# An encoder layer on one core: where the first maxima of the attention are taken, how the Fourier branch's second half is run, and which engine does the last norm

## The chip, the core and the metric

The kernel runs on one core of a Trainium2 chip. Five engines work from their own queues and meet through semaphores: TensorE (PE) multiplies matrices, VectorE (DVE) and ScalarE (ACT) do elementwise work and reductions, GpSimd (POOL) elementwise work on SBUF, and SyncE (SP) issues most DMAs. The metric is the device time of one execution in microseconds (us); less is better.

## What is computed

Two sequences of 2048 tokens ("prompt" and "sample"), 1024 wide, go through one layer with shared weights:

```python
u = _rmsnorm(h, g_norm)
z = u @ w_in                       # q | k | v | attention gate | Fourier input | Fourier gate
q = _apply_axial_rope(_rmsnorm(q, g_q), cos, sin)
k = _apply_axial_rope(_rmsnorm(k, g_k), cos, sin)
a = _blocked_gqa(q, k, v) * jax.nn.silu(ga)        # 8 q heads, 2 kv heads of 64
fo = _fourier_branch(f, w_fmix) * jax.nn.silu(gf)  # real part of a 2-D DFT, then a map per group
h = h + jnp.concatenate([a, fo], axis=-1) @ w_out
gate = jax.nn.sigmoid(_rmsnorm(h, g_ple) @ w_ple_gate)
h = h + (p @ w_ple) * gate
y = _rmsnorm(h, g_final)
```

## The kernel before

Products that need the accuracy are done as three matmuls of 16-bit halves (`mm`, L428); the attention's product with v and the DFT are done in 32 bits.

**Projections** (`project`, to about 847 us). The tokens of both sequences come in 16 chunks of 256, the prompt's eight first. `iteration(i)` issues for several chunks at once: loads and norm of a later chunk, q, k and v of this one, rotations of earlier ones, and `sweep_part`, which takes the Fourier and gate products of a chunk piece by piece (some 66 pieces). After each fifth piece it takes one step of a background generator `bg` (weights of the later stages). `bank()` hands out PSUM banks, five from the pool `psX` and three from `psF`. Orders are written out by hand: what is issued first on an engine runs first there. In this stage `self.dq` is None, so work given to `defer` is issued at once. In iteration 13 (`n - 3`), `early()` closes a pool and starts the attention generator, which loads k and v of the prompt's first kv head and the q of two units (L1076 to L1090).

**Attention** (`attention`). A unit is 128 queries of one kv head with its four q heads: 64 units, 8 steps each. Step `g` begins with `flush`, which issues what was deferred; then come the scores of step `j` of unit `u` (six matmuls on PE, L1104, two exponentials on ACT, L1107, a running sum of 128x1024 on POOL, L1112); one maximum of a unit 13 steps ahead (`maxima`: a pair of matmuls into `ps_m`, which has one buffer, L1127, and a reduction on DVE, L1131); and on each fourth step the product with v (L1162). `negate` and `max_rows` turn the eight maxima of a unit into a row (L1148) that is subtracted by the first score matmul. Because of the 13 steps (`AHEAD`), the loop starts at `g = -13`, and in the first 13 steps there is nothing but maxima.

**Fill.** `interleave` runs attention, and after each of its steps takes pieces of a second generator, `fill`, as far as a budget goes: 755 us in all, spread over the steps, with at most 5 us saved up. A piece that yields None ends the turn. The fill is the second half of the Fourier branch (`fourier2`, eight tiles for a sequence), then the output part (`outp`, 32 tiles of 128 tokens). In a tile of `fourier2`, g (g_in), gate (gf_in) and constants are loaded two tiles ahead; PE transforms over positions (L1025) and over channels (`mix`, L983), ACT copies, DVE adds and subtracts (L993), POOL multiplies by the gate (L995), and `fin`, deferred by two steps, takes the largest value on DVE (`fmax`, L999) and stores the result (`fod`, L941). `fmax` of a sequence sets a scale (`mix_max`) that the output part needs. The tiles g_in, gf_in and fo share 14 buffers. `fourier2` was called once for each sequence; each call begins with loads and three empty steps and ends when its deferred work is out (`after(self.tick, 1)`). `hook` loads one piece of the output weights twice a tile.

In `outp`, tile t is multiplied by w_out (`out1`), normed (`norm`: 16 small operations on POOL, L1363 to L1366), transposed (`out2`, which needs the norm), multiplied by the gate's weights (`out3`) and, two tiles later, scaled and stored (`out4`, L1373 on DVE and L1375 as a DMA issued by POOL). `out4` was handed to the slow queue at the seventh piece of `out3`, `out2` right after it. A tile may be prepared only when both kv heads' units of its tokens are done (`ready`).

**End.** After the last attention step the rest of the fill runs alone, `self.dq` is None again, and work is issued at once.

`defer(fn)` runs `fn` at the next flush; nested once more, it runs two flushes later. `after(ticket, more)` yields None until that flush and `more` others are over.

Of the kernel before, what the change touches and what calls it, by code (L numbers as in the profile page):

```python
# [19 lines left out]
DM = 1024  # L20
# [119 lines left out]
class Build:  # L140
    def __init__(self, ctx, tc, a, y):
# [9 lines left out]
        self.slow, self.passed, self.step = [], set(), 0  # L151
        self.nw2k = 10
# [388 lines left out]
    def project(self, P, PU, W, early, wkv, wq, wga, bg, mid):  # L541
# [216 lines left out]
        def iteration(i):  # L758
# [41 lines left out]
            if i == n + 3:  # L800
                self.drain(bg)
                for f in stores_next:
# [131 lines left out]
    def fourier2(self, s, pool, hook=lambda: None):  # L934
# [5 lines left out]
        def tiles(dma, t, y, dram, sb, load):  # L940
# [9 lines left out]
        def load_c(t):  # L950
            C[t] = pool.tile([128, 2, 128], F32, name="c2", bufs=FP + 1)
            nc.sync.dma_start(C[t][:].rearrange("p g c -> p (g c)"), self.a["c_dft2"][t])

        def load_g(t, g):
            G[t, g] = w2k("g_in")
            r = 16 * t + 8 * g
            nc.sync.dma_start(G[t, g][:], self.gd[s][r:r + 8].rearrange("r t d -> (r t) d"))
# [5 lines left out]
        def loads(t):  # L963

            if t < 8:
                todo.extend([lambda: load_c(t), lambda: load_g(t, 0), lambda: load_g(t, 1)])
            if 0 <= t - 1 < 8:
# [7 lines left out]
        def mix(t, fT, fx):  # L975
# [21 lines left out]
            def fin():  # L997
                for y in range(2):
                    nc.vector.tensor_reduce(out=self.fmax[s][:, 2 * t + y:2 * t + y + 1], in_=fo[y][:], op=ALU.max,  # L999
# [4 lines left out]
            self.tick = self.defer(lambda: self.defer(fin))  # L1004
# [12 lines left out]
        for t in range(8):  # L1017
# [17 lines left out]
            if t == 0:  # L1035
# [10 lines left out]
        yield from self.after(self.tick, 1)  # L1046
# [15 lines left out]
    def attention(self, kvp):  # L1062
# [9 lines left out]
        def load_kv(s, kv, pool):  # L1072
            for b in range(2):
                k = pool.tile([128, 4, 3, 128], F16, name="k", bufs=2)
# [3 lines left out]
            for b in range(2):  # L1078
                v = pool.tile([128, 8, 64], F32, name="v", bufs=2)
# [40 lines left out]
        def maxima(u, k):  # L1120
# [3 lines left out]
            ps = self.psM.tile([128, 1024], F32, name="ps_m")  # L1124
            for c in range(2):
                sl = slice(64 * c, 64 * c + 64)
                nc.tensor.matmul(ps[:, c * 512:(c + 1) * 512], Q[u][0][sl, h, :], kt[s, kv, half][sl, :, 0, :],  # L1127
                                 start=True, stop=True)
            if k == 0:
                MX[u] = st.tile([128, 4, 2], F32, name="a_mx", bufs=2)  # L1130
            nc.vector.reduce_max(MX[u][:, h, half:half + 1], ps[:], axis=AX.X)  # L1131
# [4 lines left out]
            nc.vector.tensor_reduce(out=m[:], in_=mx[:], op=ALU.max, axis=AX.X)  # L1136
# [7 lines left out]
        def max_rows(u):  # L1144
# [4 lines left out]
            MR[u] = mr = pool.tile([128, 4, 128], F16, name="mr", bufs=1)  # L1149
# [58 lines left out]
        load_kv(0, 0, kvp)  # L1208
        for u in range(2):
            load_q(u)  # L1210
        pool = yield 0.0
        nms = [pool.tile([128, 128], F32, name=f"nm{i}", bufs=1) for i in range(2)]
        for x in nms:
            nc.gpsimd.memset(x[:], 0.0)
        ones = pool.tile([128, 64], F32, name="ones", bufs=1)
        nc.gpsimd.memset(ones[:], 1.0)
        kone = pool.tile([128, 128], F16, name="kone", bufs=1)
        nc.gpsimd.memset(kone[:], K_ONE)
        own = pool.tile([128, 4], F32, name="own", bufs=1)
        nc.gpsimd.tensor_tensor(out=own[:], in0=self.ident[:, 0:4], in1=self.ident[:, 64:68], op=ALU.add)  # L1220
        load_kv(0, 1, pool)
        fresh = {last[0, kv]: (kv, p) for kv, p in enumerate((kvp, pool))}
        for g in range(-AHEAD, 8 * n + 7):
# [5 lines left out]
            if j == 4 and u - 1 in fresh:  # L1229
                load_kv(1, *fresh[u - 1])  # L1230
            if 0 <= u < n:
                scores(u, j)
            v, k = divmod(g + AHEAD, 8)
            if v < n:
                maxima(v, k)
            if k == 1 and 0 <= v - 1 < n:
                negate(v - 1)
# [450 lines left out]
```

## Time and profile before

| what | us |
|---|---|
| median of 3 runs | 2833.74 (2832.60 to 2834.88) |
| the profiled execution | 2832.63 |
| its span, first to last instruction | 2830.9 |
| mean granted TensorE clock | 0.982 of full speed |

The span is cut into stretches by what runs: projections to 847.2 us, the 13 lead steps to 898.0, attention with the Fourier fill to about 1045, attention with the output fill to 2748, the end of the fill to 2814.7, and 16.2 us after the last matmul. A row of a table by stretches gives for each engine the time it was busy and in brackets the number of its instructions. In an order of time, the bracket behind an instruction is the idle time of its engine just before it and what ended it. A wait is shown as "engine, what waited, <- what it waited for: us in total, times, longest".

### The profile page before, as it was taken

The numbers are of one execution on the slowest core, as the hardware profiler recorded it, in microseconds if no ns is written. First come the engines' busy times: TensorE is split into PE (matmuls) and PEld (weight loads), VectorE is DVE, ScalarE is ACT, GpSimd is POOL, SyncE is SP. The second block draws the span as 40 slices with busy tenths as digits, with TensorE's granted clock in tenths as the row PEclk, the third lists the DMA queues.
The fourth block names the chain that finished last, engine by engine and source line by source line (L and its number), as shares of the span: only waits on it lengthen the run. The fifth ranks groups of instructions, "written<-read, shape, count | busy, mean of one in ns | idle before, by whom it ended". The sixth has DMA issues, their size and how long they took to land.

```text
span 2830.9 us, 40445 instructions
## 1 busy us (share of the span) xinstructions
PE 2692.4 (95%) x15332; PEld 1190.8 (42%) x15332; DVE 1687.5 (60%) x2397; ACT 1211.3 (43%) x2047; POOL 1648.4 (58%) x1462
## 2 busy tenths in 40 slices
PE   5699999999996998999999999999999999999997
PEld 2356565655555443333333333333333333333333
DVE  7555566563445565666666666666666666666632
ACT  4333343332222454554444455444444444444441
POOL 0122333242342787777776778777776777777663
PEclk9899999999997999999999999999999999999999
DMA  7376777773439542112221223322222222222222
GB/s 217 97 207 176 198 214 182 181 182 88 130 85 327 166 129 68 51 53 73 65 59 41 66 55 83 97 60 51 75 56 65 58 70 73 53 73 70 58 58 80
DMA packets 418532, 296.43 MB, mean 105 GB/s; under 512 B 259456, under 2 KB 360128, under 8 KB 418336
## 3 DMA queue, kind: packets, MB, share of 16 engines
q1 hardware_dynamic: 405280, 251.55, 33.7%
q0 software_dynamic: 13056, 42.29, 4.2%
q8 instruction: 120, 1.97, 0.3%
q14 instruction: 76, 0.62, 0.1%
HBM read 149.56 MB, written 86.51 MB: 83 GB/s over the span
## 4 chain that ended last, share of the span: by engine, by line
PE 83%; DVE 5%; DMA 3%; issue 3%; ACT 2%; POOL 2%; SPq 1%; POOLq 0%; ACTq 0%; DVEq 0%
PE ps_f L428 34%; PE ps_o L1162 15%; PE ps_x L428 14%; PE ps_s L1104 13%; PE ps_m L1127 4%; PE ps_f L1196 1%; ACT p L1107 1%; PE ps_f L1148 1%; PE ps_f L1025 1%; POOL acc L1112 1%; PE ps_f L983 1%; PE ps_x L884 1%; DVE a_mx L1131 1%; DVE w_mx L299 0%; DVE mh L1314 0%
## 5 line engine op out<-in xcount | busy, mean ns | idle before, releaser
L1112 POOL TENSOR_TENSOR acc<-acc,p 128x1024 f32<-128x1024 f32 x384 | 913.7, 2379 | 225.9 <-ACT p L1107 171.2
L1131 DVE TENSOR_REDUCE a_mx<-ps_m 128x1 f32<-128x1024 f32 x512 | 626.0, 1223 | 593.2 <-PE ps_m L1127 592.4
L1107 ACT ACTIVATE p<-ps_s,s_scale 128x512 f32<-128x512 f32 x1024 | 647.5, 683 | 754.8 <-PE ps_s L1104 735.1
L1162 PE MATMUL ps_o<-p,v 128*64 128x512 f32 x2048 | 466.3, 597 | 0.0
L428 PEld LDWEIGHTS <-uc 128*128 128x128 f16 x3072 | 302.7, 99 | 338.1 <-DMA uc<-hl 37.8
L1104 PE MATMUL ps_s<-q,k 64*128 64x512 f16 x3072 | 432.1, 381 | 11.3 <-ACT p L1107 10.9
L428 PE MATMUL ps_f<-w_pg,hT 128*128 128x512 f16 x1464 | 350.5, 380 | 2.3 <-DMA hT<-h_hl 2.2
L1104 PEld LDWEIGHTS <-k 64*128 64x128 f16 x3072 | 118.6, 94 | 317.3 <-issue 246.7
L1162 PEld LDWEIGHTS ps_o<-p,v 128*64 128x64 f32 x2048 | 141.8, 137 | 257.8 <-issue 248.8
L1110 POOL TENSOR_TENSOR acc<-p,p 128x1024 f32<-128x1024 f32 x64 | 150.4, 2350 | 153.7 <-ACT p L1107 153.4
L428 PEld LDWEIGHTS <-hT 128*128 128x128 f16 x1536 | 138.5, 98 | 205.6 <-issue 60.8
L1127 PE MATMUL ps_m<-k,q 64*128 64x512 f16 x1024 | 200.7, 380 | 24.3 <-DVE a_mx L1131 23.8
L428 PE MATMUL ps_f<-w_wo,mh 128*128 128x512 f16 x744 | 181.6, 382 | 5.0 <-DVE mh L1314 5.0
L428 PE MATMUL ps_f<-w_wo,mT 128*128 128x512 f16 x744 | 180.1, 380 | 1.5 <-DMA mT<-mh 1.5
L428 PEld LDWEIGHTS <-w_ga 128*128 128x128 f16 x1536 | 149.9, 98 | 38.0 <-ACT w_ga L321 9.0
L901 POOL DMA_DIRECT2D gfd<-gt x32 | 19.4, 606 | 222.6 <-DVE gt L929 217.9
L1178 ACT ACTIVATE tb<-ps_o,a_scale 64x256 f32<-64x256 f32 x128 | 60.0, 469 | 169.2 <-PE ps_o L1162 168.4
L1198 DVE RECIPROCAL ps_f<-ps_f 128x256 f32<-128x256 f32 x64 | 112.4, 1756 | 12.3 <-PE ps_f L1196 12.3
L919 POOL DMA_DIRECT2D agd<-gat x64 | 35.2, 550 | 137.8 <-DVE gat L929 133.3
L428 PEld LDWEIGHTS <-mh 128*128 128x128 f16 x768 | 68.4, 98 | 111.3 <-issue 37.1
L428 PEld LDWEIGHTS <-mT 128*128 128x128 f16 x768 | 70.6, 98 | 100.1 <-issue 22.5
L428 PE MATMUL ps_x<-uc,w_ga 128*128 128x256 f16 x1008 | 112.7, 273 | 0.0
(273 smaller groups left out, 3337.2 us busy)
## 6 DMA issues: line engine op xcount, KB each, us to landing
q<-qTd SPq DMA_DIRECT2D x256, 64.0 KB, 2.2
ag<-agd SPq DMA_DIRECT2D x64, 256.0 KB, 3.2
out<-h POOLq DMA_DIRECT2D x32, 512.0 KB, 3.2
x<-in_x_prompt SPq DMA_DIRECT2D x16, 512.0 KB, 4.6
w_st<-in_w_out SPq DMA_DIRECT2D x32, 256.0 KB, 3.8
gfd<-gt POOLq DMA_DIRECT2D x32, 256.0 KB, 3.0
gd<-ge POOLq DMA_DIRECT2D x32, 256.0 KB, 3.8
agd<-gat POOLq DMA_DIRECT2D x64, 128.0 KB, 2.6
```

Of the source, the lines that this page charges most:

```text
L428: self.nc.tensor.matmul(ps, lhs(ia, k), rhs(ib, k), start=(i == 0), stop=(i == 3 * ks - 1))
L884: nc.tensor.matmul(pf[:], self.dft1[:] if t % 8 else self.dft1x[:, t // 8], F.pop(tt)[:], start=True, stop=True)
L919: nc.gpsimd.dma_start(self.agd[s][1, r * 128:(r + 1) * 128, c * n:(c + 1) * n], gt[:, :n])
L1104: nc.tensor.matmul(S[u][e][:], w[sl], q[sl].rearrange("p h q -> p (h q)"), start=j == i == 0, stop=i + 1 == len(todo), skip_group_check=True)
L1107: nc.scalar.activation(p[:, e, :], S[u][e][:], AF.Exp, scale=self.sc["s_scale"][:])
L1110: nc.gpsimd.tensor_tensor(out=ACC[u][:], in0=P[u, 0][:], in1=p[:], op=ALU.add)
L1112: nc.gpsimd.tensor_tensor(out=ACC[u][:], in0=ACC[u][:], in1=p[:], op=ALU.add)
L1127: nc.tensor.matmul(ps[:, c * 512:(c + 1) * 512], Q[u][0][sl, h, :], kt[s, kv, half][sl, :, 0, :], start=True, stop=True)
L1131: nc.vector.reduce_max(MX[u][:, h, half:half + 1], ps[:], axis=AX.X)
L1162: nc.tensor.matmul(o[64 * e:64 * e + 64, :], vt[s, kv, c // 8][:, c % 8, :], p[:, e, :], start=(j == 0), stop=(j == 7))
L1178: nc.scalar.activation(tb[64 * e:64 * e + 64], ov[64 - 64 * e:128 - 64 * e, e], AF.Copy, scale=self.sc["a_scale"][64 - 64 * e:128 - 64 * e ...
L1198: nc.vector.reciprocal(r, ps[:, 0:256])
```

## The change

- The 13 leading maxima are a generator `leads`, kept as `self.ahead`. `sweep_part` takes one step of it at every piece whose count leaves 2 when divided by 5; what is left is taken in iteration `n + 3`. A first maximum uses two banks of `psX` instead of `ps_m`, and two reductions of 512 instead of one of 1024; between its matmuls and its reductions the generator yields. The attention loop starts at `g = 0`.
- For that, k and v of both kv heads, the units' rows and small constants lie in the pool opened by `early()`, and k and v of the second head are loaded there in iteration 13.
- `fourier2` runs 16 tiles, eight of each sequence, in one call; at tile 10, when the first sequence's last `fin` is over, it yields "half", and `fill` makes the output generator. `fin` is deferred by four steps instead of two. `hook` loads one piece of the weights a tile instead of two.
- In `outp`, while attention runs, `out4` and `out2` of a tile wait until more than three flushes have passed since its `norm`.
- When attention is over, `norm` runs on DVE; the last tile is scaled in two halves, each stored by a DMA that SP issues.
- The number of steps for which the budget is spread is 13 less.

```diff
@@ sweep_part, in project
                         if len(done) % NBF == 0:
                             next(bg, None)
+                        if len(done) % NBF == 2:
+                            next(self.ahead, None)
@@ fourier2
-            self.tick = self.defer(lambda: self.defer(fin))
+            self.tick = self.defer(lambda: self.defer(lambda: self.defer(lambda: self.defer(fin))))
...
-        for t in range(8):
+        for t in range(16):
+            if t == 10:
+                yield from self.after(half, 3)
+                yield "half"
...
-            if t == 0:
+            if t % 8 == 0:
+                if t:
+                    half = self.tick
...
-        yield from self.after(self.tick, 1)
+        yield from self.after(self.tick, 3)
@@ attention
-        def maxima(u, k):
+        def maxima(u, k, first=False):
...
-            ps = self.psM.tile([128, 1024], F32, name="ps_m")
+            if first:
+                ps = [self.psX.tile([128, 512], F32, name="ps_x")[:] for _ in range(2)]
+            else:
+                pm = self.psM.tile([128, 1024], F32, name="ps_m")
+                ps = [pm[:, c * 512:(c + 1) * 512] for c in range(2)]
...
-            nc.vector.reduce_max(MX[u][:, h, half:half + 1], ps[:], axis=AX.X)
+            if first:
+                yield
+            for c, x in enumerate(ps if first else [pm[:]]):
+                nc.vector.reduce_max(MX[u][:, h, half, c:c + 1], x, axis=AX.X)
...
-        load_kv(0, 0, kvp)
-        for u in range(2):
-            load_q(u)
+        for kv in range(2):
+            load_kv(0, kv)
+            load_q(kv)
...
+        def leads():
+            for g in range(-AHEAD, 0):
+                yield from lead(g)
+                yield
+                turn(g)
+
+        self.ahead = leads()
         pool = yield 0.0
...
-        for g in range(-AHEAD, 8 * n + 7):
+        for g in range(8 * n + 7):
@@ outp
-            nc.gpsimd.tensor_scalar(out=ms[:], in0=ss[:], scalar1=1.0 / DM, scalar2=EPS, op0=ALU.mult, op1=ALU.add)
-            r = self.rsqrt(ms[:], 2, "h", nc.gpsimd)
+            e = nc.vector if self.dq is None else nc.gpsimd
+            e.tensor_scalar(out=ms[:], in0=ss[:], scalar1=1.0 / DM, scalar2=EPS, op0=ALU.mult, op1=ALU.add)
+            r = self.rsqrt(ms[:], 2, "h", e)
...
-                nc.vector.scalar_tensor_tensor(out=x[:], in0=x[:], scalar=r[:, 1:2], in1=gfin[:],
-                                               op0=ALU.mult, op1=ALU.mult)
-                nc.gpsimd.dma_start(yv[t // NT][t % NT], x[:])
+                last = t == N2 - 1
+                for i in range(1 + last):
+                    sl = slice(512 * i, 512 * i + 512 if last else DM)
+                    nc.vector.scalar_tensor_tensor(out=x[:, sl], in0=x[:, sl], scalar=r[:, 1:2], in1=gfin[:, sl],
+                                                   op0=ALU.mult, op1=ALU.mult)
+                    (nc.sync if last else nc.gpsimd).dma_start(yv[t // NT][t % NT][:, sl], x[:, sl])
...
-            t3 = t4
+            t3, tn, o4 = t4, [self.nflush], ok(t - 2)
             for i, us in enumerate(along(out3(t - 1, 1), pr) if ok(t - 1) else [0.0] * 8):
-                if i == O4 and ok(t - 2):
-                    t4 = out4(t - 2, r)
+                if o4 and i >= O4 and (self.dq is None or self.nflush > tn[0] + 3):
+                    t4, o4 = out4(t - 2, r), False
                 yield us
+            if self.dq is not None and ok(t - 1):
+                yield from self.after(tn, 3)
+            if o4:
+                t4 = out4(t - 2, r)
@@ fill, in run
                 def hook(n=1):
-                    for _ in range(n):
+                    calls.append(n)
+                    for _ in range(n if n > 1 else len(calls) % 2):
                         if wl:
                             wl.pop(0)()
...
-                yield from self.fourier2(0, B, hook)
-                out, go = self.outp(C0, ow, lambda: fill_stack.enter_context(pool("C", side="right"))), None
-                for us in self.fourier2(1, B, hook):
-                    go = go or next(out)
+                out, go = iter(()), None
+                for us in self.fourier2(B, hook):
+                    if us == "half":
+                        out = self.outp(C0, ow, lambda: fill_stack.enter_context(pool("C", side="right")))
+                        continue
+                    go = go or next(out, None)
                     yield us
```

More of the change, by code (lines that the diff above doesn't have):

```diff
@@ L151, in __init__ @@
         self.slow, self.passed, self.step = [], set(), 0
+        self.ahead = iter(())
         self.nw2k = 10
@@ L801, in iteration @@
                 self.drain(bg)
+                self.drain(self.ahead)
                 for f in stores_next:
@@ L998, in fin @@
                 for y in range(2):
[L999 removed]
+                    c = 2 * (t % 8) + y
+                    nc.vector.tensor_reduce(out=self.fmax[t // 8][:, c:c + 1], in_=fo[y][:], op=ALU.max,
                                             axis=AX.X, apply_absolute_value=True)
@@ L1118, in scores @@
                         del kt[s, kv, b]
-        def maxima(u, k):
+        def maxima(u, k, first=False):
             s, kv, t = units[u]
             h, half = k // 2, k % 2
-            ps = self.psM.tile([128, 1024], F32, name="ps_m")
+            if first:
[3 more added lines that the diff above has]
+                ps = [pm[:, c * 512:(c + 1) * 512] for c in range(2)]
             for c in range(2):
                 sl = slice(64 * c, 64 * c + 64)
-                nc.tensor.matmul(ps[:, c * 512:(c + 1) * 512], Q[u][0][sl, h, :], kt[s, kv, half][sl, :, 0, :],
-                                 start=True, stop=True)
+                nc.tensor.matmul(ps[c], Q[u][0][sl, h, :], kt[s, kv, half][sl, :, 0, :], start=True, stop=True)
             if k == 0:
-                MX[u] = st.tile([128, 4, 2], F32, name="a_mx", bufs=2)
-            nc.vector.reduce_max(MX[u][:, h, half:half + 1], ps[:], axis=AX.X)
+                MX[u] = st.tile([128, 4, 2, 2 if first else 1], F32, name="a_mx", tag=f"a_mx{int(first)}", bufs=2)
+                if first:
+                    nc.gpsimd.memset(MX[u][:], -3e38)
+            if first:
+                yield
+            for c, x in enumerate(ps if first else [pm[:]]):
+                nc.vector.reduce_max(MX[u][:, h, half, c:c + 1], x, axis=AX.X)
             if k < 7:
@@ L1206, in sums, with lead, turn @@
             self.defer(store)
-        load_kv(0, 0, kvp)
-        for u in range(2):
-            load_q(u)
-        pool = yield 0.0
-        nms = [pool.tile([128, 128], F32, name=f"nm{i}", bufs=1) for i in range(2)]
+        for kv in range(2):
+            load_kv(0, kv)
+            load_q(kv)
+        nms = [kvp.tile([128, 128], F32, name=f"nm{i}", bufs=1) for i in range(2)]
         for x in nms:
             nc.gpsimd.memset(x[:], 0.0)
+        kone = kvp.tile([128, 128], F16, name="kone", bufs=1)
+        nc.gpsimd.memset(kone[:], K_ONE)
+        own = kvp.tile([128, 4], F32, name="own", bufs=1)
+        nc.gpsimd.tensor_tensor(out=own[:], in0=self.ident[:, 0:4], in1=self.ident[:, 64:68], op=ALU.add)
+        def lead(g):
+            v, k = divmod(g + AHEAD, 8)
+            if v < n:
+                yield from maxima(v, k, g < 0)
+            if k == 1 and 0 <= v - 1 < n:
+                negate(v - 1)
+        def turn(g):
+            v, k = divmod(g + 2, 8)
+            if k == 0 and 0 <= v < n:
+                max_rows(v)
+        def leads():
[4 more added lines that the diff above has]
+        self.ahead = leads()
+        pool = yield 0.0
         ones = pool.tile([128, 64], F32, name="ones", bufs=1)
         nc.gpsimd.memset(ones[:], 1.0)
[L1217 to L1222, printed above, removed]
-        for g in range(-AHEAD, 8 * n + 7):
+        fresh = {last[0, kv]: kv for kv in range(2)}
+        for g in range(8 * n + 7):
             self.step = g
@@ L1229, in attention @@
             if j == 4 and u - 1 in fresh:
-                load_kv(1, *fresh[u - 1])
+                load_kv(1, fresh[u - 1])
             if 0 <= u < n:
                 scores(u, j)
[L1233 to L1237, printed above, removed]
+            self.drain(lead(g))
             if j == 4 and 0 <= u - 1 < n:
```

34 lines of the change are left out of this document (17 added, 17 removed).

## The prediction

> **What bounds the kernel now.** I read the page first, then a table by stretches cut at the borders of the stages, then the order of time on TensorE at the gaps.
>
> ```profile
> span 2830.9 us, 40445 instructions
> ...
> PE 2692.4 (95%) x15332; PEld 1190.8 (42%) x15332; DVE 1687.5 (60%) x2397; ACT 1211.3 (43%) x2047; POOL 1648.4 (58%) x1462
> ...
> L1112 POOL TENSOR_TENSOR acc<-acc,p 128x1024 f32<-128x1024 f32 x384 | 913.7, 2379 | 225.9 <-ACT p L1107 171.2
> L1131 DVE TENSOR_REDUCE a_mx<-ps_m 128x1 f32<-128x1024 f32 x512 | 626.0, 1223 | 593.2 <-PE ps_m L1127 592.4
> ```
>
> TensorE (PE) is busy for 95% of the span, and no other engine for more than 60%. The change leaves the number of matmuls alone, so the time can only move by what PE loses: idle time, and work done at a reduced clock. The stretches show where that is (columns: length, then busy us of PE, PEld, DVE, ACT, POOL with counts, then granted clock, DMA share, GB/s).
>
> ```profile
> 142.00:847.20 705.20, 704.54 (x4230) 419.14 (x4227) 390.93 (x878) 238.53 (x432) 241.77 (x234) 1.00 0.62 164
> 847.20:898.00 50.80, 31.33 (x215) 26.28 (x214) 27.04 (x33) 11.20 (x18) 11.72 (x15) 0.80 0.99 317
> 898.00:1045.00 147.00, 129.24 (x825) 72.72 (x825) 89.98 (x119) 72.28 (x119) 107.10 (x61) 0.92 0.57 183
> ...
> 1105.00:1480.00 375.00, 372.77 (x2091) 132.36 (x2089) 235.31 (x242) 182.97 (x306) 275.91 (x222) 1.00 0.23 60
> 1480.00:1605.00 125.00, 114.77 (x628) 40.37 (x626) 80.14 (x89) 56.80 (x95) 85.76 (x71) 0.97 0.19 51
> ...
> 2060.00:2260.00 200.00, 193.34 (x1072) 69.30 (x1068) 124.64 (x123) 92.31 (x155) 139.39 (x124) 1.00 0.24 62
> ...
> 2748.00:2814.70 66.70, 63.99 (x296) 28.04 (x292) 24.58 (x28) 15.64 (x23) 21.77 (x64) 1.00 0.35 93
> 2814.70:2830.90 16.20, 0.00 (x0) 0.00 (x0) 2.73 (x3) 1.15 (x2) 5.07 (x18) 0.56 0.08 32
> ```
>
> The projections (142 to 847) lose nothing. The 13 lead steps (847 to 898) lose 50.8 - 31.3 = 19.5 us idle. The stretch where attention runs beside the Fourier tiles (898 to 1045) loses 147 - 129.2 = 17.8 us idle and, at a mean clock of 0.92, up to 129.2 x 0.08 = 10.3 us of slow work. Later there are 10.2 us in 1480 to 1605, 6.7 us in 2060 to 2260, 2.7 us at the end of the fill, and 16.2 us after the last matmul. The gaps have names:
>
> ```profile
> 865.18 3.75 PE L1025 MATMUL ps_f<-c,g_in 128*128 128x128 f32 x16 [10.97 <-DMA g_in<-gd]
> ...
> 903.04 2.07 PE L983 MATMUL ps_f<-bd,fT 128*128 128x128 f32 x8 [3.80 <-ACT fo L987]
> ...
> 916.30 0.61 PE L1127 MATMUL ps_m<-k,q 64*128 64x512 f16 x2 [2.79 <-DVE a_mx L1131]
> ...
> 1516.28 0.61 PE L1127 MATMUL ps_m<-k,q 64*128 64x512 f16 x2 [6.08 <-DVE a_mx L1131]
> ```
>
> **Part 1, the first maxima move into the projections.** Removed: 13 steps in which attention has nothing but a maximum, so that PE waits for the Fourier branch's first load. The matmuls move to a stretch that is full, so they lengthen it:
>
> ```profile
> 874.47 0.39 PE L1127 MATMUL ps_m<-k,q 64*128 64x512 f16 x2
> 874.79 1.16 PE L983 MATMUL ps_f<-bd,fT 128*128 128x128 f32 x8
> ...
> 732.00:741.40 9.40, 9.40 (x44) 4.22 (x42) 0.00 (x0) 1.36 (x2) 0.00 (x0) 1.00 0.69 171
> ...
> 729.47 0.28 ACT L654 ACTIVATE vs<-ps_f 128x128 f32<-128x128 f32 x1 [4.01 <-DMA vd<-vs]
> ```
>
> A pair takes 874.79 - 874.47 = 0.32 us of PE, 13 pairs 4.2 us: added there, removed here, net nothing. VectorE gets two reductions of 512 for each, an estimate of 26 x 0.7 = 18 us in all from half of the 1.22 us and a little more. They go into two chunks of the projection, and in each of them VectorE has a hole like that of 732 to 741 (busy 0.00 of 9.4 us). Cost there: what could stop PE is the two of the five ps_x banks that each maximum holds until VectorE comes to it; VectorE is behind its rotations when a chunk starts. I take 1 us, with bounds 0 and 8 (two chunks, each one wait of 4.01, the size of the ACT wait above). The six loads of the second head's k and v go into SP's queue ahead of the store of vs, so that very ACT wait grows by their issue time; behind it stand ACT's copies out of PSUM, which PE reaches some banks later, so I take nothing.
>
> What PE does instead of waiting: the scores of unit 0 can start at once, without fill until the first g_in lands. The nearest stretch of attention without fill is this one:
>
> ```profile
> 1066.00:1100.00 34.00, 27.45 (x151) 9.07 (x150) 25.34 (x26) 18.47 (x32) 31.26 (x29) 1.00 0.34 93
> ...
> 855.03 1.92 SPq L1076 DMA_DIRECT2D k<-kTd  x4
> ...
> 859.79 0.82 SPq L957 DMA_DIRECT2D g_in<-gd  x2
> ...
> 865.20:898.00 32.80, 29.27 (x206) 25.81 (x206) 21.40 (x27) 10.73 (x17) 9.99 (x8) 0.91 1.00 340
> ```
>
> There PE is busy 27.45 of 34 us and POOL, with its running sum, 31.3 of 34: 19% lost. SP loses the k and v loads between 855 and 858 but gets four q loads in their place, so I keep 865.2 - 847.2 = 18 us without fill: 18 x 0.19 = 3.5 us lost. The tiles of the scores lie in memory that the projections give back, where the last stores run until after 855.03; for that I take 2 us, bounds 0 and 9. Before, the lead steps lost 19.5 us idle and 29.27 x 0.09 = 2.6 us by the clock. **Gain: 22.1 - 3.5 - 2 - 1 = 15.6, say 16 us; bounds 6 and 19.**
>
> **Part 2, one Fourier run for both sequences, its reductions later.** The second start (load, three empty steps, final wait) goes; the final wait gets two steps longer, once. The 16 weight loads are spread over 16 tiles instead of 8. The reduction fmax, which waits for POOL's product, comes four steps after the matmuls instead of two. Waits in 898 to 1045:
>
> ```profile
> L1104 PE MATMUL ps_s<-q,k 64*128 64x512 f16 x216 | 34.2, 405 | 1.6 <-ACT p L1107 1.6
> ...
> DVE fmax L999 <- POOL fo L995: 25.1, 16, 4.7
> ...
> PE ps_m L1127 <- DVE a_mx L1131: 9.9, 6, 3.2
> ...
> 902.39 0.60 ACT L987 ACTIVATE fo<-ps_f 128x512 f32<-128x512 f32 x1 [6.77 <-DMA fod<-fo]
> ...
> 915.00:920.00 5.00, 3.70 (x17) 3.26 (x17) 4.67 (x8) 0.69 (x1) 4.39 (x4) 0.56 0.96 361
> ```
>
> VectorE stands 25.1 us behind POOL, at most 4.7 us at a time; the attention's maxima are queued behind it, ps_m has one buffer, and PE loses 9.9 us. Two steps more (216 score matmuls at six a step make 36 steps in 147 us, 4 us each) are 8 us: longer than the longest wait, so this chain goes. After the gap of 2.79 us the clock is 0.56, so part of the 10.3 us goes with it. By the Trainium skill, "TensorE: Matmul & The Clock Gate", Part 1, the clock falls only after an idle window of about 3.4 us; the row shows it after less. By the page what gaps remain would cost no clock, by the row they do; the difference would be the 2 us that I leave for it. The gap of 3.80 us at 903 is ACT waiting for a buffer whose store was slow while the DMA ran at its limit (share 0.99 in 847 to 898); with half the weight loads per tile I expect less of it. Of 28.1 us I leave 10: about 4 for ACT's turns, 2 for the longer final wait (four steps at 19% of 2.4 us, one running sum on POOL, is 1.8), 2 for the clock, 2 unknown. **Gain 18 us; bounds 4 and 25.** Cover for the two weights per tile that come later: the output projection starts only after the run.
>
> **Part 3, out4 and out2 wait three steps after the norm.** In the waits of the whole page
>
> ```profile
> DVE h L1373 <- POOL rsh_z L245: 27.4, 5, 6.4
> ...
> 1510.00:1520.00 10.00, 3.92 (x14) 1.06 (x13) 6.03 (x8) 2.41 (x3) 9.48 (x12) 0.66 0.26 54
> ```
>
> only one of the five touches PE while attention runs: 10 - 3.92 = 6.1 us idle and 3.92 x 0.34 = 1.3 us by the clock. Four steps later POOL has long ended. **Gain 7 us; bounds 3 and 8.** The added wait stops the fill generator, not an engine; queued behind it is the next tile's transpose, and the budget it leaves unused, up to its cap, is spent after. I cost it at nothing while the last output matmuls of a tile outlast four steps; without that cover it is part of the 6.7 us of 2060 to 2260, which I leave as it is.
>
> **Part 4, the end.** From POOL's first operation to the last issue:
>
> ```profile
> 2817.47 0.18 POOL L1363 TENSOR_SCALAR h_ms<-h_ss 128x2 f32<-128x2 f32 x1 [7.05 <-ACT sq L1358]
> ...
> 2821.78 1.28 DVE L1373 SCALAR_TENSOR_TENSOR h<-h,rsh_z,gfin 128x1024 f32<-128x1024 f32 x1 [5.59 <-POOL rsh_z L245]
> ...
> 2823.36 0.62 POOL L1375 DMA_DIRECT2D out<-h  x1 [0.21 <-issue]
> ...
> 728.41 0.18 DVE L235 TENSOR_TENSOR rsq_t<-rsq_y 128x22 f32<-128x22 f32 x1
> ...
> 730.58 0.24 DVE L607 TENSOR_SCALAR q_rs<-rsq_z,inv_q 128x16 f32<-128x16 f32 x1
> ...
> out<-h POOLq DMA_DIRECT2D x32, 512.0 KB, 3.2
> ...
> gfd<-gt POOLq DMA_DIRECT2D x32, 256.0 KB, 3.0
> ```
>
> POOL needs 2821.78 - 2817.47 = 4.3 us. On VectorE ten such steps took 730.58 - 728.41 = 2.2 us; 14 take 3.0: 1.3 us less. Before, the issue ends 2823.98 - 2821.78 = 2.2 us after the scaling starts; two halves (about 1.4 us) and a short issue on SP come to 1.9: 0.3 less. A store of 256 KB lands 0.2 us sooner than one of 512 KB. By the Trainium skill, "DMA: Bandwidth & Descriptors", "Anatomy of one DMA", 2.0 us are fixed and the rest goes with the bytes, which would give 0.6; the rows show 0.2. The other norms of the end shorten in the same way; of the 2.7 us that PE waits there I take 1. **Gain 3 us; bounds 1 and 5.**
>
> **Sum.** 16 + 18 + 7 + 3 = 44 us. The profiled execution took 2832.63 (1.7 more than its span); 2832.6 - 44 = 2788.6, and the median of before is 1.1 above that execution: **2789 us**. About 0.2%, 5.7 us, is what a measurement of this kernel can tell from no change.
>
> **Rivals.** *Less*: in the mixed stretch ACT and the DMA simply become the next wait, and only 4 of the 18 us come: 30 in all, 2803. For it: 3.80 us for ACT fo, and POOL at 107 of 147 us. Against: the named chain is the largest. *More*: the fill starts some 20 us of work later against the attention, so it runs less often into tiles whose attention isn't done; then the 6.7 us of 2060 to 2260 and the other 4.1 of 1480 to 1605 go, and 5 of the bounds above: 44 + 16 = 60, 2773. For it: the output projection waits for named units. Against: the budget catches up in each step. *Slower*: fo is held two steps longer in the ring of 14 buffers, of which each tile takes six (2.33 tiles around). If the store isn't done when the ring comes round, loads and copies of every tile wait as at 902.39; 16 tiles at the 3.80 us that PE lost there are 61 us, 61 - 44 = 17 more than before, 2850. It decides from 12 of the 16 tiles on (12 x 3.8 = 46). For it: the wait occurred once already with the shorter hold. Against: that was with the DMA full, and loads are issued two tiles ahead. *No effect*: the wait for memory (9), banks (8) and a start of attention that stays empty eat parts 1 and 2; 2831.
>
> **Chances.** Forecast (2778 to 2798) 0.60; less 0.16; more 0.13; slower 0.06; no effect 0.05. Faster by over 0.2%: 0.60 + 0.16 + 0.13 = 0.89; within: 0.05; slower: 0.06. The range leaves out no effect, slower and the ends of less and more: 2768 to 2816.
>
> **What would show it.** Right: the 10.97 us gap gone, TensorE's clock at 1.00 near the start of attention, fmax's wait for POOL under 5 us, no 6 us gap near the second scale, 14 us after the last matmul. Wrong: gaps in the last two projection chunks, scores waiting for ACT at the start, or fod stores named as releasers.

## The result, and the profile after

| | before | after |
|---|---|---|
| median of 5 runs, us | 2833.74 (2832.60 to 2834.88) | 2786.74 (2782.22 to 2787.17) |
| profiled execution, us | 2832.63 | 2787.15 |
| its span, us | 2830.9 | 2785.4 |
| mean granted TensorE clock | 0.982 | 0.985 |

The ratio after to before is 0.9828, with a 95% interval of 0.9816 to 0.9841: 47 us faster, where the forecast was 44. The sum fits. Its terms don't, as the experiments below show: one part of the change brings nearly all of it and another costs time.

First the page of the kernel after, span and busy time:

```profile
span 2785.4 us, 40412 instructions
PE 2681.2 (96%) x15332; PEld 1181.3 (42%) x15332; DVE 1693.6 (61%) x2467; ACT 1212.6 (44%) x2047; POOL 1631.1 (59%) x1395
```

The number of matmuls is the same, 15332. PE's busy time fell by 2692.4 - 2681.2 = 11.2 us, its idle time by the other 34.3 us of the span (45.5). Only a part of the 11.2 us is the clock: an estimate, busy time times (1 - granted clock) added up over stretches of 1 us, gives 25.0 us lost to a reduced clock before and 20.8 after, 4 us less. The other 7 us of busy time have no shown cause. The table by stretches of the kernel after (columns as before):

```profile
142.00:854.70 712.70, 712.68 (x4270) 420.80 (x4267) 410.83 (x911) 239.53 (x433) 245.17 (x240) 1.00 0.62 165
854.70:869.80 15.10, 6.20 (x37) 1.90 (x35) 5.82 (x7) 5.53 (x9) 8.06 (x6) 0.80 0.88 249
869.80:994.00 124.20, 118.02 (x834) 71.71 (x835) 75.82 (x102) 69.25 (x114) 86.67 (x49) 0.98 0.72 226
994.00:1004.00 10.00, 4.36 (x14) 1.52 (x15) 7.02 (x8) 0.98 (x1) 9.92 (x7) 0.51 0.55 171
...
1480.00:1605.00 125.00, 122.73 (x682) 43.54 (x681) 79.22 (x79) 59.29 (x99) 94.87 (x92) 0.99 0.22 60
1605.00:2060.00 455.00, 450.05 (x2505) 160.74 (x2503) 282.46 (x293) 218.05 (x363) 329.58 (x279) 1.00 0.27 68
...
2260.00:2702.00 442.00, 437.77 (x2426) 156.97 (x2424) 265.36 (x275) 212.43 (x354) 317.46 (x280) 1.00 0.24 63
...
2775.60:2785.40 9.80, 0.01 (x1) 0.00 (x0) 4.90 (x18) 1.15 (x2) 0.00 (x0) 0.65 0.14 54
```

The projections grew by 7.5 us and stayed full (712.68 of 712.70). The start of attention, 854.70 to 869.80, loses 8.9 us. In 869.80 to 994.00 the clock is 0.98, where the stretch of before (898 to 1045) had 0.92, but at its end a hole of about 10 us begins, and in 994.00 to 1004.00 the clock is 0.51. The tail is 9.8 us instead of 16.2. The gaps by name, from the order of time of the kernel after:

```profile
863.95 0.92 PE L1143 MATMUL ps_m<-k,q 64*128 64x512 f16 x2 [2.09 <-DMA q<-qTd]
869.78 2.47 PE L1035 MATMUL ps_f<-c,g_in 128*128 128x128 f32 x10 [4.92 <-DMA g_in<-gd]
...
981.25 0.38 POOL L1291 PARTITION_ALL_REDUCE mx4r<-mx  x1 [6.13 <-ACT tb L1198]
...
989.83 2.33 POOL L1124 TENSOR_TENSOR acc<-acc,p 128x1024 f32<-128x1024 f32 x1 [8.20 <-issue]
...
995.85 1.42 DVE L999 TENSOR_TENSOR fo<-ps_f,fo 128x512 f32<-128x512 f32 x2 [10.23 <-DMA gf_in<-gfd]
...
999.64 0.61 PE L1143 MATMUL ps_m<-k,q 64*128 64x512 f16 x2 [10.38 <-DVE a_mx L1151]
```

The 10.97 us gap is gone, but two smaller ones for loads take its place (2.09 and 4.92). The 10.38 us gap is new. Ahead of it POOL does nothing for 8.20 us, and no other engine is named as the reason: that idle time follows the all-reduce over partitions, which is shown with 0.38 us. From POOL to PE the trace names this chain: the load of gf_in is issued only when a product of POOL has freed a buffer of the ring of 14 (SP waits 9.5 us for that), VectorE stands 10.23 us until the load is there, and PE waits for the maximum behind it. So the ring carries the delay.

### The profile page after: what moved, and what is told of

Same layout as the page of the kernel before. It is cut to its first block, busy times and chain, and to the rows that moved or that the text cites. A ratio compares the mean times of both kernels' runs of the same rounds, so it can differ in the third digit from the quotient of the medians.

```text
span 2785.4 us, 40412 instructions
## 1 busy us (share of the span) xinstructions
PE 2681.2 (96%) x15332; PEld 1181.3 (42%) x15332; DVE 1693.6 (61%) x2467; ACT 1212.6 (44%) x2047; POOL 1631.1 (59%) x1395
## 4 chain that ended last, share of the span: by engine, by line
PE 91%; DVE 4%; DMA 2%; ACT 1%; issue 1%; POOL 1%; SPq 0%; DVEq 0%; ACTq 0%; POOLq 0%
PE ps_f L429 37%; PE ps_x L429 17%; PE ps_o L1182 15%; PE ps_s L1116 14%; PE ps_m L1143 4%; PE ps_f L1216 1%; PE ps_f L1035 1%; PE ps_f L989 1%; PE ps_f L1168 1%; PE ps_x L888 1%; ACT p L1119 1%; DVE w_mx L300 0%; DMA hT<-h_hl 0%; DVE a_mx L1151 0%; DVE h_hl L1425 0%
## 5 line engine op out<-in xcount | busy, mean ns | idle before, releaser
L1151 DVE TENSOR_REDUCE a_mx<-ps_m 128x1 f32<-128x1024 f32 x499 | 610.4, 1223 | 596.2 <-PE ps_m L1143 595.6
L1116 PE MATMUL ps_s<-q,k 64*128 64x512 f16 x3072 | 424.8, 379 | 4.6 <-ACT p L1119 4.5
L1143 PE MATMUL ps_m<-k,q 64*128 64x512 f16 x998 | 192.3, 377 | 16.8 <-DVE a_mx L1151 14.6
```

What stands on the lines that cost most here:

```text
L1116: nc.tensor.matmul(S[u][e][:], w[sl], q[sl].rearrange("p h q -> p (h q)"), start=j == i == 0, stop=i + 1 == len(todo), skip_group_check=True)
L1143: nc.tensor.matmul(ps[c], Q[u][0][sl, h, :], kt[s, kv, half][sl, :, 0, :], start=True, stop=True)
L1151: nc.vector.reduce_max(MX[u][:, h, half, c:c + 1], x, axis=AX.X)
```

## The experiments

### Each part alone

The hunks of the diff above, one part at a time on the kernel before; a core line of each:

```diff
 part 1: sweep_part, the drain, attention, interleave
+                        if len(done) % NBF == 2:
+                            next(self.ahead, None)
 part 2: fourier2 and its call in fill
+        for t in range(16):
 part 3: out4 and out2 in outp
+                if o4 and i >= O4 and (self.dq is None or self.nflush > tn[0] + 3):
 part 4: norm and the last tile's store
+                    (nc.sync if last else nc.gpsimd).dma_start(yv[t // NT][t % NT][:, sl], x[:, sl])
```

> The kernel before with the first maxima moved into the projections and nothing else. The prediction's sum: 16 us less than before (2818). Rival, from the two traces: the stretch between the last projection and the first Fourier matmul still loses about 9 of its 15 us, so only about 12 us come (2822). Second rival, parts lean on each other: with the old Fourier run, 16 weight loads over 8 tiles and the DMA full, the maxima's gain is lost to the loads and under 6 us remain (over 2828).

> The kernel before with one Fourier run for both sequences, weight loads spread, and the reduction two steps later; maxima, norm waits and end as before. The prediction's sum: 18 us less (2816). Rival, from the trace after, where one gap of 10.4 us came in beside the Fourier tiles: about 10 us less (2824), with a gap of 8 us or more near POOL's reduction over partitions.

> The kernel before with only the three steps between norm and out4 or out2. The prediction's sum: 7 us less (2827), the gap of 6.1 us near 1516 us gone. Rival: the wait moves fill to later places, where it meets tiles that are not ready, and gives back 4 us or more (2830 to 2834).

> The kernel before with only the norm on VectorE at the end and the last tile stored in two halves by SP. The prediction's sum: 3 us less (2831). Rival, from the trace after, where 9.8 us instead of 16.2 follow the last matmul and PE waits for nothing in the end: 8 to 9 us less (2825).

| kernel | median, us | ratio to before (95%) | against 2833.08 |
|---|---|---|---|
| part 1 alone | 2787.59 | 0.9836 (0.9821 to 0.9851) | -45.5 |
| part 2 alone | 2829.44 | 0.9982 (0.9973 to 0.9992) | -3.6 |
| part 3 alone | 2836.43 | 1.0014 (1.0002 to 1.0026) | +3.3 |
| part 4 alone | 2825.18 | 0.9970 (0.9958 to 0.9982) | -7.9 |

Only part 4 came out as expected, by its rival (2825). Part 1 gained far more than its sum or either rival, part 2 less than both, and part 3 lost more than its rival. The intervals are wide against the small ones: they allow 2.3 to 7.6 us of gain for part 2 and 0.6 to 7.4 us of loss for part 3.

Part 1 is as fast alone as the whole change. To see how, the tables by stretches of before and of part 1 alone, cut at the last matmul of the Fourier tiles (1036.75 and 1045.10) and 65 us behind it. Before:

```profile
847.20:1036.75 189.55, 153.95 (x1004) 96.46 (x1004) 110.49 (x143) 80.73 (x133) 110.95 (x71) 0.88 0.69 221
...
1036.75:1101.75 65.00, 55.84 (x306) 19.19 (x307) 42.91 (x45) 29.20 (x50) 52.60 (x40) 1.00 0.30 87
1101.75:1480.00 378.25, 376.02 (x2106) 133.82 (x2104) 235.31 (x242) 182.97 (x306) 275.91 (x222) 1.00 0.23 61
```

Part 1 alone:

```profile
854.28:1045.10 190.82, 167.95 (x1143) 97.55 (x1144) 116.96 (x151) 98.51 (x162) 138.56 (x79) 0.93 0.67 214
1045.10:1110.10 65.00, 60.84 (x337) 21.81 (x339) 41.20 (x44) 28.96 (x47) 53.31 (x42) 1.00 0.38 112
...
1480.00:1605.00 125.00, 123.27 (x696) 43.92 (x694) 80.50 (x81) 59.43 (x99) 96.58 (x92) 1.00 0.22 60
...
2060.00:2260.00 200.00, 196.83 (x1092) 70.76 (x1093) 125.91 (x127) 93.83 (x156) 139.26 (x114) 1.00 0.25 68
```

The first stretch takes as long as before (190.82 and 189.55 us) but holds 139 matmuls more. Its idle time falls from 35.6 to 22.9 us, by 12.7. From there to 2260 us before lost 9.2 + 2.2 + 10.2 + 6.7 = 28.3 us idle; in part 1 alone the rows shown lose 4.2, 1.7 and 3.2, 9.1 in all, and the stretches between them 0.2. With 0.8 from there to the end of attention (0.1 before) that is 18.3 us less than before, far from the place that the part edits. PE's busy time is 12.9 us less (2679.5 on the page of part 1 alone); by the same estimate as above 7.5 of it are the clock (25.0 us lost before, 17.5 now), and 5.4 have no shown cause. So the 45.2 us between the spans are 12.7 of idle time at the start, 18.3 of idle time later, 12.9 of busy time, and 1.3 of idle time in the projections and behind the attention.

Part 2's chain is real and breaking it helps little. Waits of PE and VectorE in the mixed stretch (898 to 1037 before, 898 to 1050 in part 2 alone), before:

```profile
PE ps_m L1127 <- DVE a_mx L1131: 8.9, 5, 3.2
...
DVE fmax L999 <- POOL fo L995: 24.8, 15, 4.7
```

and in part 2 alone:

```profile
PE ps_m L1135 <- DVE a_mx L1139: 14.7, 7, 7.4
...
DVE fo L995 <- POOL fo L997: 7.1, 1, 7.1
```

The wait of fmax is gone, as forecast. But PE waits longer for VectorE than before, 14.7 us instead of 8.9, half of it at once: there VectorE stands 7.1 us behind POOL with another instruction of the Fourier tiles. In part 1 alone fmax still waits, by the waits of its whole page,

```profile
DVE fmax L1003 <- POOL fo L999: 28.0, 22, 8.0
```

and that kernel is 45 us faster nonetheless. So the row with the largest sum was not the one that cost the time.

Part 3 removed a gap that another part removes too: in part 1 alone the 6.08 us gap near 1516 is gone (1480 to 1605 loses 1.7 us) with out4 and out2 where they were. Alone it did remove it, and made other waits. Waits of the whole page, part 3 alone:

```profile
PE ps_f L428 <- DMA hT<-h_hl: 9.4, 5, 2.8
...
PE ps_f L428 <- DVE mh L1314: 7.4, 6, 2.0
```

Before, the same two waits were 2.2 and 5.0 us: 9.6 us more. These are the operands of a tile's matmuls, which come late when the tile starts late. 9.6 us more against the gap of 6.1 that is gone leaves 3.5, close to the 3.3 measured.

### Two parts, and all but one

```diff
 parts 1 and 4: both sets of hunks; the rest of before
 without part 3, on the kernel after:
-            t3, tn, o4 = t4, [self.nflush], ok(t - 2)
+            t3 = t4
...
-                if o4 and i >= O4 and (self.dq is None or self.nflush > tn[0] + 3):
-                    t4, o4 = out4(t - 2, r), False
+                if i == O4 and ok(t - 2):
+                    t4 = out4(t - 2, r)
...
-            if self.dq is not None and ok(t - 1):
-                yield from self.after(tn, 3)
```

> The kernel before with the moved maxima and the new end, the Fourier runs and the norm waits as before. If the parts add as they measured alone (45.5 and 7.9 us), about 2780, some 6 us below the changed kernel. Rival: the end's gain is partly the same time as the first part's (the fill that runs after the attention), then 2783 to 2787, like the changed kernel.

> The changed kernel without the three steps between norm and out4 or out2. Theory, from part 3 alone (3.3 us slower, with TensorE waiting for the transpose of the normed tile): 2783, some 3 to 5 us below the changed kernel, and no wait for hT over 1 us between 1600 and 2700. Rival, the prediction's: the waits hide a late norm, and without them a gap of some 6 us comes back near the second scale: 2790 or more.

Parts 1 and 4 together: 2778.36 us, ratio 0.9799 (0.9783 to 0.9815); they add up (45.5 + 7.9 = 53.4 would give 2780). Without part 3: 2776.07 us, 0.9793 (0.9777 to 0.9809). The two can't be told apart, so part 2 on top of parts 1 and 4 brought nothing that these runs resolve. But without part 3 is 10.7 us below the whole change, better than both expectations: in company part 3 costs more than the 3.3 us that it costs alone. Stretches without part 3:

```profile
1605.00:2060.00 455.00, 454.88 (x2548) 163.10 (x2546) 289.12 (x298) 223.26 (x370) 336.00 (x282) 1.00 0.27 70
...
2260.00:2698.87 438.87, 438.57 (x2433) 157.50 (x2432) 259.77 (x271) 212.03 (x352) 320.47 (x289) 1.00 0.24 63
```

It loses 0.1 and 0.3 us there. The kernel after, with part 3, loses 5.0 and 4.2 (rows at the top). Its waits name the reason:

```profile
PE ps_f L429 <- DMA hT<-h_hl: 6.4, 4, 2.5
```

Without part 3 there is no such row, and the wait for mh is 1.4 us instead of 4.5: 9.5 us less in the two. In company the gap that part 3 would remove is gone already by part 1, and the whole cost remains.

### Is the gain of part 1 where the fill lies?

Count the score matmuls from the end of the projections to the last Fourier matmul, six a step. Groups by line, before:

```profile
L1104 PE MATMUL ps_s<-q,k 64*128 64x512 f16 x205 | 32.3, 407 | 1.0 <-ACT p L1107 1.0
```

and parts 1 and 4:

```profile
L1108 PE MATMUL ps_s<-q,k 64*128 64x512 f16 x284 | 42.6, 389 | 2.9 <-ACT p L1111 2.9
```

205 / 6 = 34 steps of attention were done before when the Fourier tiles ended, 284 / 6 = 47 with part 1. The output fill so starts 13 steps further into the attention, where more units are done. The next edit takes most of that back: on parts 1 and 4, the fill's share in the first 30 steps is raised, with the number of steps that the rest is spread over set to match, and nothing else is edited.

```diff
-FIRST, SLOW = 30, 0.85
+FIRST, SLOW = 30, 1.35
...
-            self.interleave(att(), f, FILL, 8 * 64 * (PVG - 1) // PVG * (1 + RATE) / 2 + 7 * RATE)
+            self.interleave(att(), f, FILL, 8 * 64 * (PVG - 1) // PVG * (1 + RATE) / 2 + 11 + 7 * RATE)
```

> The kernel with moved maxima and new end (2778), with the fill given 1.35 instead of 0.85 of a step's budget in the first 30 steps, so that it runs some 19 us of work ahead again, as it did when it began 13 steps before the scores. Theory: about half of what the first part gained is that the fill comes later against the attention, so its tiles meet ready units and the norm misses POOL's reduction; then some 10 us of idle time come back after 1100 us (at 1480 to 1605 and 2060 to 2260) and the time is 2786 to 2795. Rival: the gain is all at the start of the attention; then 2775 to 2780 and under 7 us idle between 1100 and 2260.

Measured: 2801.61 us, 0.9879 (0.9863 to 0.9895), 23 us above parts 1 and 4 and slower than even the theory said. The group and the stretches of this kernel, the first:

```profile
L1108 PE MATMUL ps_s<-q,k 64*128 64x512 f16 x230 | 33.9, 378 | 4.3 <-ACT p L1111 4.3
```

and the second:

```profile
853.64:1024.89 171.25, 149.24 (x1029) 92.44 (x1030) 103.25 (x137) 86.16 (x141) 120.47 (x72) 0.94 0.75 239
1089.89:1480.00 390.11, 385.06 (x2161) 136.91 (x2161) 251.14 (x264) 191.92 (x320) 282.92 (x225) 1.00 0.22 57
1480.00:1605.00 125.00, 116.84 (x651) 41.56 (x649) 77.28 (x79) 57.49 (x97) 95.47 (x78) 1.00 0.21 56
...
2060.00:2260.00 200.00, 190.91 (x1050) 68.91 (x1048) 126.98 (x124) 93.11 (x154) 137.01 (x112) 1.00 0.27 66
```

The Fourier tiles end after 230 / 6 = 38 steps, 9 of the 13 steps earlier. The start of attention is no worse than in parts 1 and 4 (22.0 us idle, there 20.8). But the idle time further on is back: 5.1, 8.2 and 9.1 us in the rows shown. The same three stretches in parts 1 and 4:

```profile
1104.61:1480.00 375.39, 375.27 (x2113) 133.13 (x2111) 239.60 (x259) 185.76 (x311) 276.32 (x227) 1.00 0.23 59
1480.00:1605.00 125.00, 123.36 (x695) 44.05 (x696) 81.85 (x81) 61.34 (x103) 96.89 (x87) 1.00 0.22 60
...
2060.00:2260.00 200.00, 196.85 (x1091) 71.18 (x1090) 125.57 (x129) 95.39 (x159) 139.23 (x112) 1.00 0.24 64
```

0.1, 1.6 and 3.2: 22.4 against 4.9. Over all stretches from the last Fourier matmul to the end of attention it is 28.3 against 10.0, and before the change it was 28.4: the edit gives back the whole 18.3. PE's waits name it. Whole page, parts 1 and 4:

```profile
PE ps_s L1108 <- ACT p L1111: 7.2, 20, 0.8
...
PE ps_f L429 <- DVE mh L1340: 1.3, 1, 1.3
```

and with the fill ahead:

```profile
PE ps_s L1108 <- ACT p L1111: 16.7, 47, 1.0
...
PE ps_f L429 <- DVE mh L1340: 8.0, 5, 1.8
```

The scores wait for the exponentials 47 times instead of 20, as they do at the start of attention, where there is no fill yet, and the operand mh of output tiles comes late. So where the fill lies against the attention does set this idle time, and it is the larger share of what part 1 gains in idle time. Two things move together here: with more of the budget spent early, each later step also gets a smaller share (755 / 432 instead of 755 / 421 us, before 755 / 434), and no run tells the two apart. That the turns come back empty because a tile waits for its units is the likely way; the trace doesn't show the generator, so that step stays argued. The other 11 us between the two spans are busy time (2686.2 and 2675.1), of which the clock, by the estimate above, makes 2.7.

### Can the start of attention be mended?

On the kernel after: the first q of the third unit is loaded during the projections, and the fill waits eight empty steps instead of three for its first load. The core lines:

```diff
+        load_q(2, (0,))
...
-        for _ in range(3):
+        for _ in range(8):
             yield None
```

> The changed kernel with the q of the third unit loaded with the first two and eight empty steps instead of three ahead of the first Fourier tile, so that no Fourier matmul is issued before its data is there. Theory: the 8.9 us that TensorE loses between the last projection and the first Fourier matmul are two named waits (2.1 for q, 4.9 for g_in) and come down to the 19% of a stretch without fill: about 5 us less, 2782. Rival: the engine is held by the exponentials and by POOL in any case, and the fill that starts later is owed: 2786 to 2788.

A miss: 2791.40 us, 0.9849 (0.9834 to 0.9863), no gain over the kernel after, rather a loss. The table by stretches:

```profile
855.76:1052.36 196.60, 175.94 (x1185) 101.43 (x1186) 120.35 (x154) 103.18 (x170) 147.07 (x84) 0.94 0.67 210
```

Both gaps at the start are gone: from 855.76 to 872.00 PE loses 3.2 of 16.2 us. But the stretch loses 20.7 us idle, as the kernel after does in its own (854.76 to 1040.12). The order of time shows the loss at another place, behind the all-reduce at 984.64 and the work that POOL has to make up for:

```profile
1004.72 1.15 ACT L1345 ACTIVATE mh<-ag,mix_s 128x1024 f16<-128x1024 f32 x1 [10.04 <-POOL ag L1331]
...
1006.50 0.79 PE L1035 MATMUL ps_f<-c,g_in 128*128 128x128 f32 x2 [8.48 <-ACT fT L1037]
```

### The hole behind the all-reduce

On the kernel after, the maxima over partitions are taken without POOL: a transpose by TensorE, a reduction by VectorE, a product with the identity, and a matmul with ones that spreads the result.

```diff
-            nc.gpsimd.partition_all_reduce(mm[:, 0:3], m[:, 0:3], 128, bass_isa.ReduceOp.max)
+        nc.tensor.matmul(ps[:, 0:128], self.mxz[:], self.ident[:], start=True, stop=True)
+        nc.vector.tensor_reduce(out=r[:], in_=ps[:, 0:128], op=ALU.max, axis=AX.X)
+        nc.vector.tensor_scalar(out=self.mxd[:], in0=self.ident[:], scalar1=r[:], scalar2=None, op0=ALU.mult)
...
+        nc.tensor.matmul(ps[:, 0:128], self.mxo[:], self.mxd[:], start=True, stop=True)
+        nc.vector.tensor_copy(mm[:], ps[:, 0:4])
```

> The changed kernel with the two reductions over partitions of the scale done by a transposing matmul, a VectorE maximum and a second matmul with ones, instead of POOL's instruction. Theory: the gap of 10.4 us near 1000 us follows POOL's 8 us of standing still behind that instruction, so it goes, and the one of 2.3 us near 1498 too: 2776 or less. Rival: the gap comes from the ring of 14 buffers in which fo is held four steps; then it stays, shifted, and the time is 2784 to 2787.

2778.87 us, 0.9804 (0.9789 to 0.9819), 7.9 us below the kernel after, between theory and rival; the two intervals just overlap, but each of its runs is faster than each of the kernel after. The order of time at the hole:

```profile
991.28 0.61 PE L1143 MATMUL ps_m<-k,q 64*128 64x512 f16 x2 [3.93 <-DVE a_mx L1151]
```

The gap fell from 10.38 to 3.93 us, and the 2.3 us that PE lost in 1480 to 1605 are gone. The edit also hands the scale on some 4 us later, which can't have helped. With POOL's instruction the result isn't what is late: in part 2 alone it ends at 961.89, VectorE goes on with its result at once,

```profile
961.92 0.27 DVE L1271 TENSOR_SCALAR mxb<-mx4r,va_i 128x1 f32<-128x1 f32 x1 [3.80 <-POOL mx4r L1265]
```

and POOL's next work starts at 969.26, after 7.37 us.

The Trainium skill, "GPSIMD Engine Reference", "When to use GPSIMD", calls GpSimd the only option for a reduction across partitions. For this one, of three columns, the runs show another that costs less.

Without part 3 and with this edit, both diffs as above:

> The changed kernel without the norm waits and with the scale's reductions on TensorE and VectorE. If the two add as they measured on the changed kernel (10.7 and 7.9 us): 2768, and faster than every kernel so far. Rival: both take the same stalls away, then 2774 to 2777.

2766.18 us (2765.53 to 2766.59), 0.9758 (0.9743 to 0.9772): below both kernels, and the two savings add up (10.7 + 7.9 = 18.6 of the 20.6 us below the kernel after). Here each of the two is clear of the intervals: 9.9 us below the kernel without part 3, and 12.7 us below the one with this edit and part 3.

### Two steps or four for fmax

On the kernel without part 3, fin is deferred by two steps as before the change, the one run of 16 tiles kept.

```diff
-            self.tick = self.defer(lambda: self.defer(lambda: self.defer(lambda: self.defer(fin))))
+            self.tick = self.defer(lambda: self.defer(fin))
...
-                yield from self.after(half, 3)
+                yield from self.after(half, 1)
...
-        yield from self.after(self.tick, 3)
+        yield from self.after(self.tick, 1)
```

> The changed kernel without the norm waits (2776), with the reduction fmax two steps after the matmuls again instead of four. The prediction's chain: VectorE waits some 25 us for POOL again, TensorE loses about 10 us to it, 2784 or more. Rival, from part 1 alone, where that wait was there (28.0 us) and the loss of the stretch not much larger: 2774 to 2779.

2782.00 us, 0.9815 (0.9801 to 0.9830): 6 us above the kernel without part 3, between the two expectations, with intervals that overlap. Its waits and its order of time, the first:

```profile
DVE fmax L1006 <- POOL fo L1001: 36.0, 19, 15.7
```

and the second:

```profile
1000.71 0.61 PE L1143 MATMUL ps_m<-k,q 64*128 64x512 f16 x2 [14.14 <-DVE a_mx L1151]
```

fmax waits up to 15.7 us, at the all-reduce, and PE's hole there is 14.14 us, where the kernel without part 3 has one of 11.15. That the longer deferral is worth something isn't shown beyond noise; what the trace shows of it lies at that one place.

### The last store

On part 4 alone, both halves are stored by POOL's queue:

```diff
-                    (nc.sync if last else nc.gpsimd).dma_start(yv[t // NT][t % NT][:, sl], x[:, sl])
+                    nc.gpsimd.dma_start(yv[t // NT][t % NT][:, sl], x[:, sl])
```

> The kernel before with the new end (2825), but the two halves of the last tile stored by POOL's queue instead of SP's. Theory, from the two traces, in which the span ends 6.9 us after the end of POOL's last issue and 2.7 us after SP's: the queue is worth about 4 us, so 2829. Rival: halves and norm make the gain, the queue nothing: 2825 to 2826.

2832.03 us, 0.9995 (0.9985 to 1.0004): the gain of part 4 is gone. The stretch after the last matmul, part 4 alone:

```profile
2816.03:2825.70 9.67, 0.00 (x1) 0.00 (x0) 4.90 (x18) 1.15 (x2) 0.00 (x0) 0.65 0.15 54
```

and with POOL's queue, with the issue in the order of time behind it:

```profile
2818.43:2832.90 14.47, 0.00 (x0) 0.00 (x0) 4.91 (x18) 1.15 (x2) 1.09 (x2) 0.63 0.10 36
```

```profile
2824.76 1.21 POOL L1379 DMA_DIRECT2D out<-h  x2 [11.88 <-DVE h L1377]
```

VectorE does the same (4.90 and 4.91 us). With POOL's queue the issue is over at 2825.97 and the program ends 6.9 us later, as before the change (2823.98 to 2830.9). In the kernel after, SP does it:

```profile
2778.48 0.17 DVE L1398 TENSOR_SCALAR h_ms<-h_ss 128x2 f32<-128x2 f32 x1 [1.27 <-ACT sq L1392]
...
2780.91 1.41 DVE L1411 SCALAR_TENSOR_TENSOR h<-h,rsh_z,gfin 128x512 f32<-128x512 f32 x2
2781.68 1.00 SPq L1413 DMA_DIRECT2D out<-h  x2
```

Its issue is over at 2782.68 and the program ends 2.7 us later. Of the 6.9 us between the two medians the tail accounts for 14.47 - 9.67 = 4.8; the other 2 lie earlier and are within the spread of the runs (2821.10 to 2828.14 and 2829.22 to 2835.32).

## Why the prediction was right, and where it was not

The time came out within 3 us, by terms that were wrong and made up for each other: 16, 18, 7 and 3 us were forecast, 45.5, 3.6, -3.3 and 7.9 measured for the parts alone. That is luck. Of the signs of being right, the gap of 10.97 us, the wait of fmax, the gap near the second scale and the shorter tail (9.8 us, 14 were said) came; the clock of 1.00 near the start of attention did not (0.80, then 0.98, then 0.51).

**Part 1, 16 us with bounds 6 and 19: 45.5.** The step that failed is the bounds: they price the lead steps and the first 18 us of attention and nothing that follows. The later place of the fill stood among the rivals, *more*, but with the other parts' terms kept beside it and 4.1 and 6.7 us as its size; measured, the idle time after the Fourier tiles fell by 18.3 us, and the edit that moved the fill back returned it. It belonged to part 1 and into the sum. Even the small terms at the start were off: "18 x 0.19 = 3.5 us lost" left out the loads. The kernel after lost 8.9 of 15.1 us there: in the order of time a matmul that waits for a load (q of the third unit, 2.09; g_in, 4.92) holds the scores behind it. With both waits out of the way it lost 3.2 of 16.2, 20% and close to the 19% taken. For the good, busy time fell by 12.9 us, of which some 7.5 by the clock; the sum had 2.6.

**Part 2, 18 us with bounds 4 and 25: 3.6, at the lower bound.** The mechanism was right, fmax no longer waits for POOL. The step that failed is "So this chain goes ... of 28.1 us I leave 10": VectorE goes in order, and its next instruction that needs POOL then waits in place of fmax (7.1 us in part 2 alone). PE's wait for VectorE in that stretch did not fall (8.9 before, 14.7 in part 2 alone). Of the 10 left, the shares I gave (ACT, final wait) are not what the holes were: the largest, 7.4 and in the whole change 10.38 us, lies behind the all-reduce.

**Part 3, 7 us with bounds 3 and 8: 3.3 slower alone, some 10.7 slower in company.** The step that failed is "I cost it at nothing while the last output matmuls of a tile outlast four steps". They don't: hT and mh come later, 9.6 us of waits more alone. And the 6.1 us credited was no property of the norm: the gap is gone in part 1 alone too, where the fill stands elsewhere at that moment.

**Part 4, 3 us with bounds 1 and 5: 7.9.** The mechanism was right and a size was wrong. The norm on VectorE takes 2780.91 - 2778.48 = 2.4 us instead of 4.3, 1.9 less where I had 1.3. The term "halves by SP", 0.3 for the issue and 0.2 for the landing, was the wrong one: the end of the program follows SP's issue after 2.7 us and POOL's after 6.9. I had looked at how soon a store lands, and not at how long the program goes on after the issue of its last one, for which the trace of before had the number.

**The rivals.** *Slower* didn't come: the longer hold in the ring of 14 made nothing slower that the runs show, and four steps were if anything better than two (2776 and 2782). But the ring does carry the hole behind the all-reduce to VectorE, in one place and not in each tile. *No effect* was wrong for the sum and nearly right for part 2.

**The sum itself.** 2833.74 - 44 is 2789.7, where the last line says 2789; nothing hangs on it. The lower bound of part 1 doesn't follow from its own terms: with 9 for the memory and 8 for the banks, 22.1 - 3.5 - 9 - 8 is 1.6 and not 6.

**What stays open.** Whether the idle time that the moved fill brings back is the wait for units, and what of it is the smaller share of each later step; the part of PE's shorter busy time that isn't the clock; whether part 2 adds anything to parts 1 and 4 (0.9793 and 0.9799).

## What to carry to other kernels

When a change lets the main work start earlier beside a fill with dependences of its own, work out where the fill will stand against it from then on; here that was worth more than the gap that was removed. Before a wait is credited because its row is large, ask which instruction on the same in-order engine needs the same producer next, and before a gap is credited, whether another part of the change moves it. Where several parts are changed at once, time each of them alone even if the total fits: here one part cost 10.7 us that the total didn't show.

## What the runs showed of the hardware that was not expected

- POOL stands still behind an all-reduce over partitions: 0.38 us are shown for the instruction and 8.20 us of idle time without a named reason follow. In all twelve kernels that have it, two each, 6.6 to 9.9 us of idle time follow and 5.8 to 8.3 us go ahead of it. The result is there at once (row of part 2 alone above), so POOL isn't still working on it; what it does in that time isn't shown. Avoiding it on POOL was worth 7.9 us on the kernel after and 9.9 without part 3.
- A program whose last store is issued by POOL ended 6.9 us after the issue (five kernels), one whose last store is issued by SP 2.6 to 2.7 us after (nine kernels). The Trainium skill, "DMA: Bandwidth & Descriptors", "Latency and other measured facts", gives about 0.6 us to the first byte for SP's kind of queue and about 1 for POOL's, a difference of 0.4. That is another span than the one here, from the last issue to the end of the program, in which the runs show a difference of 4.2.
